# Banded tap matrices loaded from memory instead of built on GpSimd, and the modulation's dot products moved

## The chip, the cores and the metric

The kernel runs on one core of a Trainium2 chip. The metric is the device time of one execution in microseconds. Engines are named as in the profile: PE is TensorE (matmuls), PEld its weight load, DVE VectorE, ACT ScalarE, POOL GpSimd, SP SyncE, whose queue issues nearly all transfers from memory.

## The reference

Two layers over 512 latent tokens of 1024 features; each layer is a token mixer and a SwiGLU feed-forward block. The mixer of layer 0 is a gated linear attention that also reads 256 context tokens, the mixer of layer 1 a convolution module. Every sub-layer is normalised and modulated by vectors that come from the condition `c`.

```python
for i in range(2):
    mod_lat = silu(c) @ w_mod[i] + b_mod[i]          # 6 vectors of 1024
    sh1, sc1, gt1, sh2, sc2, gt2 = split(mod_lat, 6)
    h = modulate(rmsnorm(x, norm_mix_g[i]), sh1, sc1)
    y = gla(h, h_ctx) if i == 0 else conv_module(h)
    x = x + gt1 * y
    x = x + gt2 * swiglu(modulate(rmsnorm(x, norm_ffn_g[i]), sh2, sc2), w_in[i], w_out[i])
return rmsnorm(x, final_norm_g)

def conv_module(h):                                  # 31 taps, one filter per channel
    u = h @ w_pw1 + b_pw1
    u = u[:, :1024] * sigmoid(u[:, 1024:])
    u = depthwise_conv(u, w_dw) + b_dw
    return silu(layernorm(u)) @ w_pw2 + b_pw2
```

## The kernel before

Activations lie transposed: 8 tiles `x` of 128 features by 512 tokens. Every matrix product is done in three matmuls (`mm3`, L95 to L97): weights and activations are split into a rounded high part and the rest (`wh`, `wl`; for activations `hi`, `lo`), high times high, high times rest, rest times high. A weight chunk of 128x1024 comes by one transfer into a raw tile `wr` (three buffers), ACT casts it to `wh` (L110), DVE subtracts to get `wl` (L111); `wh` and `wl` have four buffers each. SP issues transfers in program order, and one that waits for its buffer holds back those behind it.

The order of stages is: start and attention (to about 320 us), its output projection, the feed-forward block of layer 0 (`ffn(0)`: 22 pairs of column blocks in `pairs`, then `out_proj`), the convolution module, and the feed-forward block of layer 1 (`ffn(1)`). `ffn(0)` is ordered by a scheduler, the convolution by lists written by hand (`mix`).

Between two stages stands a norm. When the tokens of one half (256) are complete, `rstd_y` sums squares on PE (L158), DVE turns the sums into reciprocal roots by eight tiny instructions on 128x2 elements (L164 and, in `newton`, L183 to L190), PE spreads them over partitions (`spread`, L170), and DVE with ACT makes the next stage's input: L197 (input times scale, the spread value read from PSUM), ACT L198, DVE L199 (which makes the low part from two tiles in SBUF). Then the other half follows. The last of `out_proj`'s eight column blocks is done in halves, so that the first half's norm can run beside the second half's matmuls.

The modulation vectors are dot products on DVE: `mod_jobs` is a generator whose every step multiplies one loaded 128x1024 tile `wm` of `w_mod` with `silu(c)` and accumulates into a column of `dots` (L229), then loads the next tile into the only `wm` buffer. After every eighth dot POOL adds the bias (L233). `step(n)` takes n steps; before, `ffn(0)` calls `step(3)` after each of 20 pairs, until none is left.

In the convolution, three of eight channel tiles (`PCH` = 4, 5, 6) are convolved on PE. For this each needs 36 banded 128x128 matrices of taps; four lie in one 128x512 tile, so there are 9 tiles a channel tile and 27 in all. Before, POOL builds them right after `ffn(0)` (L1128) by multiplying a mask of 32 diagonals (`m32`) with the taps (`wph`), one instruction for each tile:

```python
pool.tensor_tensor(tt.rearrange("p (a b) -> p a b", b=32), m32.unsqueeze(1).to_broadcast([P, 16, 32]),
                   w.unsqueeze(2).to_broadcast([P, 16, 32]), op=ALU.mult)
```

The tiles take buffers of kind `s`, of which `ffn(0)` has used all 36 until its `out_proj` has read them. PE reads the matrices in `pe_lane`, from about 820 us on.

Of the kernel before, what the change touches and what calls it, by code (L numbers as in the profile page):

```python
# [7 lines left out]
F32 = mybir.dt.float32  # L8
# [8 lines left out]
ALU = mybir.AluOpType  # L17

P = 128
D = 1024  # L20
KC = D // P
SEQ = 512
CTX = 256
HID = 2816
HC = HID // P
# [9 lines left out]
PCH = (4, 5, 6)  # L35
NF = 4
NSH = 9
# [18 lines left out]
def hybrid_kernel(ctx: ExitStack, tc: tile.TileContext, t: dict):  # L56
    nc = tc.nc
    act, dve, pool, pe, sp = nc.scalar, nc.vector, nc.gpsimd, nc.tensor, nc.sync

    cst = ctx.enter_context(tc.tile_pool(name="cst", bufs=1))  # L60
# [25 lines left out]
    def bt(tag, dt=F32):  # L86
        if tag in "cd":
            return wide(tag, dt)[:, 2:514]
        return big.tile([P, 512], dt, tag=tag, bufs=NBUF[tag], name=nm(tag))
# [127 lines left out]
    def mod_jobs():  # L217

        ij = [(0, j) for j in range(16, 48)] + [(1, j) for j in range(48)]

        def load(i, j):
            raw = wts.tile([P, 1024], F32, tag="wm", bufs=1, name=nm("wm"))
            sp.dma_start(raw, t["wmod"][i, j])
            return raw
        raw = load(*ij[0])
        yield
        for n, (i, j) in enumerate(ij):
            o = i * 48 + j
            dve.scalar_tensor_tensor(raw, raw, 1.0, sil, op0=ALU.mult, op1=ALU.mult, accum_out=dots[:, o:o + 1])  # L229
            if n + 1 < len(ij):  # L230
                raw = load(*ij[n + 1])
            if j % 8 == 7:
                pool.tensor_tensor(mod[i][:, j - 7:j + 1], dots[:, o - 7:o + 1],  # L233
                                   col(C_BMOD + o - 7, 8), op=ALU.add)
            yield

# [2 lines left out]
    def step(n):  # L239
        for _ in range(n):  # L240
            if next(jobs, 0) == 0:
                return
# [695 lines left out]
            if beside:  # L938
                beside(i)

    def ffn(i, h_, gt2, nx, after):
        sT = []

        def evac(j, po, c0, c1):
            n = c1 - c0
            if c0 == 0:
                tag = "s" if j < 18 else "c" if j < 20 else "d"
                sT.append((bt(tag, F32R), bt(tag, F32R)))
            hi, lo = sT[j]
            a = bt("t")  # L950
            act.activation(a[:, :n], po[0][:, :n], AF.Silu)
            dve.tensor_tensor(a[:, :n], a[:, :n], po[1][:, :n], op=ALU.mult)  # L952
            act.copy(hi[:, c0:c1], a[:, :n])  # L953
            dve.tensor_tensor(lo[:, c0:c1], a[:, :n], hi[:, c0:c1].bitcast(F32), op=ALU.subtract)

        pairs(f"wf{i}", HC, h_, evac, lambda i: step(3))
        r = resid(gt2)

        def ev2(m, p_, c0, c1):
            r(m, p_, c0, c1)  # L960
            nx.add(m, xs[m], c0, c1)

        out_proj(f"wo{i}", HC, sT, ev2, nx.tail, after)

# [14 lines left out]

    def after2(hf):  # L980
        if hf == 0:
            step(100)
            make_a(acol[:, 24:32], mod[1][:, 8:16], col(C_GMIX + 8, 8))
            make_a(acol[:, 32:40], mod[1][:, 32:40], col(C_GFFN + 8, 8))
        in2(hf)

    ffn(0, in1.h, mod[0][:, 40:48], n2, after2)


    HALF = WID // 2  # L990
# [128 lines left out]

    toep, ug, pe_ps, scr = {}, {}, {}, {}  # L1120

    def toeplitz(m, tag="s"):

        c = (m - PCH[0]) * 4 * NSH * NF
        for i in range(0, 4 * NSH, 4):
            tt = bt(tag)
            w = wph[:, c + i * NF:c + (i + 4) * NF]
            pool.tensor_tensor(tt.rearrange("p (a b) -> p a b", b=32), m32.unsqueeze(1).to_broadcast([P, 16, 32]),  # L1128
                               w.unsqueeze(2).to_broadcast([P, 16, 32]), op=ALU.mult)
            for j in range(4):  # L1130
                toep[m, (i + j) // NSH, (i + j) % NSH] = tt[:, j * P:(j + 1) * P]

# [184 lines left out]
    def bias2(k):  # L1317
        act.activation(xs[k], xs[k], AF.Identity, bias=gb2[:, k:k + 1])
# [32 lines left out]
            ev3(m, p_, *halves[hf])  # L1351

    ev3 = closing(mod[1][:, 16:24], n3)
    m32 = cst.tile([P, 32], F32, name="m32")
    sp.dma_start(m32, t["m32"])
    bph = cst.tile([P, 4 * len(PCH)], F32, name="bph")
    sp.dma_start(bph, t["bph"])
    wph = bt("g")
    sp.dma_start(wph[:, :len(PCH) * 4 * NSH * NF], t["wph"])
    for m in range(KC):  # L1360
        if m in PCH:
            toeplitz(m)
        else:
            cv_new(m)
    uw = {0: pair_load(0), 1: pair_load(1)}
    prod = wts.tile([P, 1024], F32, tag="wm", bufs=1, name=nm("wm"))
# [2 lines left out]
    with tc.manual_schedule(engines={E.Activation, E.DVE, E.Pool, E.PE}):  # L1369
        pool_lane = pool_order()  # L1370
        dve_start, dve_lane = dve_order()
        warm(AF.Sigmoid)
        po.update({(i, h): pair_mm(uw[i], *h) for h, i in ((h0, 0), (h0, 1), (h1, 0))})
        evc(0, po[0, h0], *h0)
        mix(dve_start[0],
            at=[(0.4, lambda: evc(1, po[1, h0], *h0)), (0.7, lambda: uw.update({2: pair_load(2)}))])
        evc(0, po[0, h1], *h1)
        po[1, h1] = pair_mm(uw[1], *h1)
        po[2] = pair_mm(uw[2], 0, SEQ)
        mix(take(pool_lane, 5), dve_start[1], at=[(0.7, lambda: evc(1, po[1, h1], *h1))])  # L1380
        for p in range(1, 7):
            def evac():
                if p > 1:
                    need(ORD[p])
                    po[ORD[p + 1]] = pair_mm(uw[p + 1], 0, SEQ, range(4))

            def second():
                if p > 1:
                    pair_mm(uw[p + 1], 0, SEQ, range(4, KC), po[ORD[p + 1]])

            def load():
                if p + 2 < KC:
                    uw[p + 2] = pair_load(ORD[p + 2])
            at = [(0.04, evac), (0.25, load), (0.5, second)]
            if p >= 3:
                at += [(0.6, lambda: bias2(2 * p - 6)), (0.8, lambda: bias2(2 * p - 5))]
            if p == 3:
                at += [(SH[0], shift_sums), (SH[1], shift_bc), (SH[2], shift_copy)]
            if p >= 5:
                at += [(0.3, lambda: to_groups(ORD[p]))]  # L1400
            mix(take(pool_lane, PN[p - 1]), take(dve_lane, DN[p - 1]), at=at)
        mix(pe_lane(4), take(pool_lane, PN[6]), take(dve_lane, DN[6]),
            at=[(N6, lambda: need(6)), (N6, lambda: to_groups(6)), (0.3, lambda: load2(0)), (0.7, lambda: load2(1))])
        pe_store(4)
        mix(pe_lane(5), take(pool_lane, PN[7]), take(dve_lane, DN[7]),
            at=[(0.3, lambda: load2(4, "s")), (0.9, lambda: pe_back(4, dve))])
        pe_store(5)
        warm(AF.Silu)
        mix(pe_lane(6), pool_lane, dve_lane, at=[(0.1, lambda: load2(2)), (0.2, lambda: load2(3))])
        cv_new(6)  # L1410
        pe_out(6, 0, act)
        pe_out(6, 1, act)
        pool.tensor_tensor(cv[6][0:64], cv[6][0:64], ncb[0:64], op=ALU.add)
        ln_open()
        pe_out(6, 2, dve)
        pe_out(6, 3, dve)
        pe_back(5, act)
        ks = (1, 0, 2, 3, 4, 7, 5, 6)
        for k in ks:
            run(ln_sums(k, 0, k == ks[-1]))  # L1420
        b = [f for k in ks for f in ln_sums(k, 1, k == ks[-1])]
        run(take(b, S1))
        ln_stat(0)
        ln_bc(0)
        run(take(b, S2))
        lane = ln_lane(0)
        run(take(lane, 5))

        def rest():
            run(b)  # L1430
            run(lane)
            ln_stat(1)
        first = pw2(range(4), 0, {1: rest, BC: lambda: ln_bc(1)})
        load2(5, "s")
        lane = ln_lane(1)
        run(take(lane, L1))
        pw2_out(first, 0)
        run(lane)
        pw2_out(pw2((4, 5), 0), 0)
        pw2_out(pw2(range(4), 1), 1)  # L1440
        load2(6)
        load2(7)
        pw2_out(pw2((4, 5), 1), 1)
# [16 lines left out]
            (sp, act)[k // 2 % 2].dma_start(t["out"][k:k + 2, :, c0:c1].rearrange("k p c -> p k c"),  # L1460
                                            y.rearrange("p (k c) -> p k c", k=2))

    ffn(1, in3.h, mod[1][:, 40:48], n4, final)

# [14 lines left out]
def phases(w):  # L1481

    import numpy as np
    pad = NF * MID + NF - 1 - WID // 2
    wp = np.pad(w, ((pad, pad), (0, 0)))
    r, d, f = np.ogrid[:NF, :NSH, :NF]
    a = wp[NF * d + r - f + NF - 1].reshape(NF, NSH, NF, KC, 4, 32)[:, :, :, list(PCH)]
    return np.ascontiguousarray(a.transpose(0, 5, 3, 4, 1, 2)).reshape(P, -1)


def layout(x, c, ctx, c_ctx, w_mod, b_mod, norm_mix_g, norm_ffn_g, gla_w_in, gla_wa_f, gla_ba_f,
# [4 lines left out]
    a = {}  # L1496
# [21 lines left out]
    tt = np.arange(512)  # L1518
    a["pmask"] = np.ascontiguousarray((np.arange(P)[:, None] > (tt % P)[None]).astype(f32))
    a["ident"] = np.eye(P, dtype=f32)  # L1520
    a["m32"] = np.ascontiguousarray(np.tile(np.eye(32, dtype=f32), (4, 1)))
    b = conv_b_dw[0].reshape(KC, 4, 32)[list(PCH)].reshape(-1, 32).T
    a["bph"] = np.ascontiguousarray(np.tile(b, (NF, 1)))
    a["wph"] = phases(conv_w_dw[0])
    a["wgo"] = _units(gla_w_out[0])
    a["wp1"] = _pairs(conv_w_pw1[0])
    a["wp2"] = _units(conv_w_pw2[0])
# [21 lines left out]
```

## Time and profile before

| | us |
|---|---|
| three runs: median (lowest, highest) | 1287.11 (1284.47, 1287.29) |
| the profiled execution, its own time | 1287.67 |
| its span from first to last instruction | 1285.7 |
| PE busy in it | 1234.1 |
| DVE busy | 734.7 |
| ACT busy | 475.8 |
| POOL busy | 226.9 |

The profiled execution's time is 1.97 us above its span and 0.56 us above the median of the runs. PE is busy nearly all the time, so a gain can come only from the places where it waits or where its clock is low; those are found by stretch, not by the sums over the whole.

### The profile page before, as it was taken

What the parts mean: (1) busy time and instruction counts of PE and PEld (TensorE: products, weight loads), DVE (VectorE), ACT (ScalarE), POOL (GpSimd) and SP (SyncE); (2) the same over time, 40 slices, a digit from 0 to 9 for tenths busy, and PEclk for the clock granted to TensorE, in tenths of its full rate; (3) what the DMA queues carried; (4) which work ended last, traced back from release to release, by engine and by line L of the source; (5) the groups of instructions that cost most, each with busy time, mean ns of one, the idle gap of its engine ahead of it and who ended that gap; (6) DMA issues with size and microseconds to landing.
All of it is one profiled execution on the core that took longest, in us unless ns stands there. A gap on an engine that the chain in (4) does not pass through costs nothing.

```text
span 1285.7 us, 17000 instructions
## 1 busy us (share of the span) xinstructions
PE 1234.1 (96%) x6692; PEld 1069.6 (83%) x6692; DVE 734.7 (57%) x1279; ACT 475.8 (37%) x748; POOL 226.9 (18%) x191
## 2 busy tenths in 40 slices
PE   8899899999899999999999699999999999999997
PEld 7678799898898888877888598889988888888886
DVE  2997976747775545545532889986733333332223
ACT  3245655443342222222222368855422222222220
POOL 0032211122200000000011859933000000000110
PEclk7999999999899999999999899999999999999999
DMA  7642542235456666556633123321143333333321
GB/s 277 223 132 74 164 147 83 83 99 149 141 167 196 193 186 196 194 166 205 195 112 101 50 66 95 117 85 65 55 128 99 97 95 95 93 95 100 93 72 66
DMA packets 54180, 162.34 MB, mean 126 GB/s; under 512 B 6226, under 2 KB 12242, under 8 KB 54100
## 3 DMA queue, kind: packets, MB, share of 16 engines
q1 hardware_dynamic: 52436, 159.16, 39.8%
q10 hardware_dynamic: 1664, 2.10, 0.5%
q8 instruction: 52, 0.85, 0.3%
q14 instruction: 28, 0.23, 0.1%
HBM read 157.83 MB, written 3.41 MB: 125 GB/s over the span
## 4 chain that ended last, share of the span: by engine, by line
PE 67%; DVE 16%; DMA 9%; issue 4%; ACT 3%; POOL 0%; DVEq 0%; ACTq 0%; POOLq 0%
PE pm L95 18%; PE pm L97 18%; PE pm L96 18%; DMA wm<-wmod 8%; DVE g L253 3%; DVE pa L1088 2%; DVE wl L111 2%; DVE wm L229 2%; PE pm L366 1%; PE pm L367 1%; PE pm L368 1%; ACT wh L110 1%; PE pa L620 1%; PE pm L527 1%; DVE pm L1088 1%
## 5 line engine op out<-in xcount | busy, mean ns | idle before, releaser
L97 PE MATMUL pm<-h,wl 128*128 128x512 f32 (+1 forms) x1008 | 373.3, 372 | 4.9 <-DVE wl L111 2.8
L96 PE MATMUL pm<-h,wh 128*128 128x512 f32 (+1 forms) x1008 | 372.1, 371 | 2.8 <-DVE h L199 2.8
L95 PE MATMUL pm<-h,wh 128*128 128x512 f32 (+1 forms) x1008 | 371.9, 372 | 0.2 <-ACT wh L110 0.2
L111 DVE TENSOR_TENSOR wl<-wr,wh 128x1024 fp32r<-128x1024 f32 (+1 forms) x176 | 224.6, 1280 | 256.9 <-ACT wh L110 255.0
L110 ACT CAST wh<-wr 128x1024 fp32r<-128x1024 f32 (+2 forms) x197 | 200.3, 1025 | 421.6 <-PE pm L96 398.8
L97 PEld LDWEIGHTS pm<-h,wl 128*128 128x128 f32 x1008 | 191.0, 190 | 39.2 <-DVE wl L111 4.4
L96 PEld LDWEIGHTS pm<-h,wh 128*128 128x128 f32 x1008 | 191.1, 190 | 35.2 <-DVE h L199 3.4
L95 PEld LDWEIGHTS pm<-h,wh 128*128 128x128 f32 x1008 | 190.1, 190 | 31.7 <-ACT wh L110 0.7
L95 PE MATMUL pm<-s,wh 128*128 128x512 f32 (+1 forms) x540 | 187.2, 347 | 1.1 <-ACT s L1271 1.1
L96 PE MATMUL pm<-s,wh 128*128 128x512 f32 (+1 forms) x540 | 186.8, 346 | 0.3 <-DVE s L278 0.2
L97 PE MATMUL pm<-s,wl 128*128 128x512 f32 (+1 forms) x540 | 186.0, 345 | 0.0
L229 DVE SCALAR_TENSOR_TENSOR wm<-wm,sil 128x1024 f32<-128x1024 f32 x80 | 102.0, 1275 | 129.1 <-DMA wm<-wmod 129.0
L885 POOL TENSOR_TENSOR g<-g,g 128x512 f32<-128x512 f32 (+1 forms) x31 | 39.8, 1283 | 488.4 <-ACT g L883 487.6
L96 PEld LDWEIGHTS pm<-s,wh 128*128 128x128 f32 x540 | 103.6, 192 | 13.1 <-DVE s L278 0.9
L95 PEld LDWEIGHTS pm<-s,wh 128*128 128x128 f32 x540 | 103.6, 192 | 13.2 <-ACT s L1271 1.3
L97 PEld LDWEIGHTS pm<-s,wl 128*128 128x128 f32 x540 | 103.6, 192 | 11.8
L111 POOL TENSOR_TENSOR wl<-wr,wh 128x1024 fp32r<-128x1024 f32 x21 | 53.1, 2541 | 198.7 <-ACT wh L110 198.7
L233 POOL TENSOR_TENSOR mod<-dots,cols 128x8 f32<-128x8 f32 x10 | 4.4, 443 | 277.6 <-DVE wm L229 277.6
L1088 DVE SCALAR_TENSOR_TENSOR pa<-s,cols,pa 128x503 f32<-128x503 f32 (+18 forms) x80 | 52.8, 701 | 0.6
L898 DVE SCALAR_TENSOR_TENSOR x<-pm,mod,x 128x256 f32<-128x256 f32 (+1 forms) x44 | 25.7, 601 | 47.5 <-PE pm L97 47.5
L953 ACT CAST s<-t 128x512 fp32r<-128x512 f32 (+1 forms) x40 | 23.1, 578 | 48.2 <-DVE t L952 48.2
L366 PE MATMUL pm<-wh,h 128*128 128x256 f32 x128 | 37.0, 289 | 0.0
(266 smaller groups left out, 1588.2 us busy)
## 6 DMA issues: line engine op xcount, KB each, us to landing
wr<-wf SPq DMA_DIRECT2D x88, 512.0 KB, 4.3
wm<-wmod SPq DMA_DIRECT2D x80, 512.0 KB, 3.7
wr<-wo SPq DMA_DIRECT2D x32, 512.0 KB, 3.7
wr<-wp SPq DMA_DIRECT2D x24, 512.0 KB, 3.9
s<-wmod SPq DMA_DIRECT2D x24, 256.0 KB, 5.5
wr<-wv SPq DMA_DIRECT2D x12, 512.0 KB, 4.1
wr<-wo SPq DMA_DIRECT2D x16, 384.0 KB, 3.3
wr<-wgo SPq DMA_DIRECT2D x8, 512.0 KB, 4.0
```

Of the source, the lines that this page charges most:

```text
L95: pe.matmul(out, wh, xh, start=start, stop=False)
L96: pe.matmul(out, wh, xl, start=False, stop=False)
L97: pe.matmul(out, wl, xh, start=False, stop=stop)
L110: act.copy(hi[:, :n], raw[:, :n])
L111: lo_eng.tensor_tensor(lo[:, :n], raw[:, :n], hi[:, :n].bitcast(F32), op=ALU.subtract)
L229: dve.scalar_tensor_tensor(raw, raw, 1.0, sil, op0=ALU.mult, op1=ALU.mult, accum_out=dots[:, o:o + 1])
L253: dve.scalar_tensor_tensor(junk, wt, 1.0, vec, op0=ALU.mult, op1=ALU.mult, accum_out=dsum[:, o:o + 1])
L366: pe.matmul(o, a, wh[:, w], start=k == 0, stop=False)
L885: pool.tensor_tensor(self.acc[:, c0:c1], self.acc[:, c0:c1], s[:, c0:c1], op=ALU.add)
L898: dve.scalar_tensor_tensor(xs[m][:, c0:c1], p_[:, :c1 - c0], gate[:, m:m + 1], xs[m][:, c0:c1], op0=ALU.mult, op1=ALU.add)
L953: act.copy(hi[:, c0:c1], a[:, :n])
L1088: dve.scalar_tensor_tensor(p_[:, lo:hi], u_sb[m][:, lo + s:hi + s], wcol(m, j), p_[:, lo:hi], op0=ALU.mult, op1=ALU.add)
```

## The change

Four things. (1) The 27 tiles of banded matrices are laid out in memory on the host (`banded`) and loaded by SP, 256 KB each, nine at a time after the pairs p = 1, 2 and 3 of the convolution; POOL's 27 multiplications, the mask and the compact taps go. (2) The modulation's bias is added by DVE and no longer by POOL. (3) `ffn(0)` calls `step(2)` after each pair and `step(1)` after each block of its `out_proj`, in place of `step(3)` and a final `step(100)`. (4) The last eight dot products, those of the second feed-forward's gate, are done in `ffn(1)`, one after each of eight pairs; their tiles come through the ring of three raw weight buffers `wr`.

```diff
         for n, (i, j) in enumerate(ij):
             o = i * 48 + j
+            if (i, j) >= (1, 40):
+                raw = load_raw(t["wmod"][i, j])
             dve.scalar_tensor_tensor(raw, raw, 1.0, sil, op0=ALU.mult, op1=ALU.mult, accum_out=dots[:, o:o + 1])
-            if n + 1 < len(ij):
+
+            if n + 1 < len(ij) and ij[n + 1] < (1, 40):
                 raw = load(*ij[n + 1])
             if j % 8 == 7:
-                pool.tensor_tensor(mod[i][:, j - 7:j + 1], dots[:, o - 7:o + 1],
+                dve.tensor_tensor(mod[i][:, j - 7:j + 1], dots[:, o - 7:o + 1],
                                    col(C_BMOD + o - 7, 8), op=ALU.add)
...
-        pairs(f"wf{i}", HC, h_, evac, lambda i: step(3))
+        pairs(f"wf{i}", HC, h_, evac, beside)
...
+            if beside2 and c0 == 0:
+                beside2()
...
-            step(100)
...
-    ffn(0, in1.h, mod[0][:, 40:48], n2, after2)
+    bph = cst.tile([P, 4 * len(PCH)], F32, name="bph")
+    sp.dma_start(bph, t["bph"])
+
+    ffn(0, in1.h, mod[0][:, 40:48], n2, after2, lambda i: step(2), lambda: step(1))
...
-    def toeplitz(m, tag="s"):
-
-        c = (m - PCH[0]) * 4 * NSH * NF
+    def toeplitz(m):
+
         for i in range(0, 4 * NSH, 4):
-            tt = bt(tag)
-            w = wph[:, c + i * NF:c + (i + 4) * NF]
-            pool.tensor_tensor(tt.rearrange("p (a b) -> p a b", b=32), m32.unsqueeze(1).to_broadcast([P, 16, 32]),
-                               w.unsqueeze(2).to_broadcast([P, 16, 32]), op=ALU.mult)
+            tt = bt("s")
+            sp.dma_start(tt, t["toep"][PCH.index(m), i // 4])
...
     for m in range(KC):
-        if m in PCH:
-            toeplitz(m)
-        else:
+        if m not in PCH:
             cv_new(m)
...
+            if p <= len(PCH):
+                at += [(0.35, lambda: toeplitz(PCH[p - 1]))]
...
-    ffn(1, in3.h, mod[1][:, 40:48], n4, final)
+    ffn(1, in3.h, mod[1][:, 40:48], n4, final, lambda i: step(1))
```

The order of PE's and ACT's instructions is the same in both kernels. That of three others moves.

POOL, from the end of `ffn(0)` to the first sum of the convolution, before (`g` are sums of squares, `s` the banded tiles, `m` the mask, `c` and `d` the convolution's outputs):

```order
L885 TENSOR_TENSOR g_5131<-g_5131,g_5575 128x512
L885 TENSOR_TENSOR g_5131<-g_5131,g_5664 128x512
L1128 TENSOR_TENSOR s_5968<-m_5950,g_5954 128x512
...
L1128 TENSOR_TENSOR s_5986<-m_5950,g_5954 128x512
L1052 COPY c_5956<-ones 128x2
```

and now:

```order
L888 TENSOR_TENSOR g_5085<-g_5085,g_5544 128x512
L888 TENSOR_TENSOR g_5085<-g_5085,g_5636 128x512
L1060 COPY c_5927<-ones 128x2
L1061 COPY c_5927<-ones 128x2
L1060 COPY c_5930<-ones 128x2
```

All 27 multiplications are gone from between the last sum of squares and the first addition of the convolution.

SP, in the convolution, before: only the weights `wp` of the first pointwise product, two chunks for each pair.

```order
L101 DMA wr_6369<-wp 128x1024
L101 DMA wr_6435<-wp 128x1024
L101 DMA wr_6441<-wp 128x1024
L101 DMA wr_6528<-wp 128x1024
L101 DMA wr_6534<-wp 128x1024
```

Now (the first and last of each group of nine):

```order
L101 DMA wr_6286<-wp 128x1024
L101 DMA wr_6370<-wp 128x1024
L1134 DMA s_6295<-toep 128x512
...
L1134 DMA s_6311<-toep 128x512
L101 DMA wr_6376<-wp 128x1024
L101 DMA wr_6481<-wp 128x1024
L1134 DMA s_6386<-toep 128x512
...
L1134 DMA s_6402<-toep 128x512
L101 DMA wr_6487<-wp 128x1024
```

The first group stands between the two chunks of pair 4, the second between those of pair 5, and the third behind the second chunk of pair 5, ahead of pair 6.

DVE, near the end of `ffn(0)`'s pairs, before (L111 a weight's low part, L229 a dot product, L952 and L954 the evacuation of a pair):

```order
L954 TENSOR_TENSOR s_4730<-t_4731,s_4729 128x512
L111 TENSOR_TENSOR wl_4833<-wr_4830,wh_4832 128x1024
L229 SCALAR_TENSOR_TENSOR wm_4580,dots<-wm_4580,sil 128x1024
L111 TENSOR_TENSOR wl_4905<-wr_4902,wh_4904 128x1024
L229 SCALAR_TENSOR_TENSOR wm_4584,dots<-wm_4584,sil 128x1024
L952 TENSOR_TENSOR t_4810<-t_4810,pm_4759 128x512
L111 TENSOR_TENSOR wl_4911<-wr_4908,wh_4910 128x1024
```

and now:

```order
L957 TENSOR_TENSOR s_4685<-t_4686,s_4684 128x512
L231 SCALAR_TENSOR_TENSOR wm_4918,dots<-wm_4918,sil 128x1024
L231 SCALAR_TENSOR_TENSOR wm_4921,dots<-wm_4921,sil 128x1024
L111 TENSOR_TENSOR wl_4851<-wr_4848,wh_4850 128x1024
L955 TENSOR_TENSOR t_4762<-t_4762,pm_4711 128x512
L111 TENSOR_TENSOR wl_4857<-wr_4854,wh_4856 128x1024
```

The two dots of a pair now stand together, behind the evacuation, and none is left between the two low parts of one pair. Until `out_proj`'s first block is added to `x` there are 48 dots of this generator in `ffn(0)` now, and 51 before.

## Rows read from the trace of the kernel before

**Rows 1.** The page: busy time by engine, and POOL's busy tenths in 40 slices.

```profile
PE 1234.1 (96%) x6692; PEld 1069.6 (83%) x6692; DVE 734.7 (57%) x1279; ACT 475.8 (37%) x748; POOL 226.9 (18%) x191
...
POOL 0032211122200000000011859933000000000110
```

**Rows 2.** The page: the chain of work that ended last, by line.

```profile
PE pm L95 18%; PE pm L97 18%; PE pm L96 18%; DMA wm<-wmod 8%; DVE g L253 3%; DVE pa L1088 2%; DVE wl L111 2%; DVE wm L229 2%; PE pm L366 1%; PE pm L367 1%; PE pm L368 1%; ACT wh L110 1%; PE pa L620 1%; PE pm L527 1%; DVE pm L1088 1%
```

**Rows 3.** PE's waits, 690 to 760 us: total, times, longest.

```profile
PE pa L170 <- DVE sm L190: 9.2, 2, 5.1
PE pm L96 <- DVE h L199: 2.8, 3, 2.3
```

**Rows 4.** Windows: length; busy (instructions) of PE, PEld, DVE, ACT, POOL; granted clock; DMA.

```profile
708.00:710.00 2.00, 0.15 (x2) 0.00 (x0) 1.93 (x3) 0.00 (x0) 2.00 (x3) 1.00 0.00 0
...
734.00:736.00 2.00, 0.00 (x0) 0.00 (x0) 1.93 (x3) 0.00 (x0) 2.00 (x3) 0.50 0.00 0
...
738.00:740.00 2.00, 2.00 (x11) 2.00 (x11) 2.00 (x4) 1.15 (x3) 2.00 (x3) 0.50 0.03 8
...
742.00:744.00 2.00, 2.00 (x19) 2.00 (x18) 2.00 (x7) 1.31 (x3) 0.00 (x0) 1.00 0.00 0
```

**Rows 5.** Timeline of DVE, 690 to 765 us: start, length.

```profile
706.54 0.16 DVE L164 TENSOR_SCALAR sm<-pa 128x2 f32<-128x2 f32 x1 [1.43 <-PE pa L158]
...
712.25 0.97 DVE L190 SCALAR_TENSOR_TENSOR sm<-sm,sm 128x2 f32<-128x2 f32 x1
714.54 1.26 DVE L197 SCALAR_TENSOR_TENSOR t<-x,acol,pa 128x256 f32<-128x256 f32 x3 [1.31 <-PE pa L170]
...
728.81 1.26 DVE L199 SCALAR_TENSOR_TENSOR h<-t,mod,h 128x256 fp32r<-128x256 f32 x1
...
735.05 0.97 DVE L190 SCALAR_TENSOR_TENSOR sm<-sm,sm 128x2 f32<-128x2 f32 x1
737.33 1.27 DVE L197 SCALAR_TENSOR_TENSOR t<-x,acol,pa 128x256 f32<-128x256 f32 x3 [1.31 <-PE pa L170]
```

**Rows 6.** Timeline of POOL, the same stretch.

```profile
705.13 10.08 POOL L1128 TENSOR_TENSOR s<-m,g 128x512 f32<-128x512 f32 x10 [5.15 <-PE pm L96]
...
724.31 17.08 POOL L1128 TENSOR_TENSOR s<-m,g 128x512 f32<-128x512 f32 x15
```

**Rows 7.** Timeline of DVE at the norm ahead of `ffn(1)`.

```profile
903.67 0.16 DVE L164 TENSOR_SCALAR sm<-pa 128x2 f32<-128x2 f32 x1 [1.72 <-PE pa L158]
...
905.05 0.16 DVE L190 SCALAR_TENSOR_TENSOR sm<-sm,sm 128x2 f32<-128x2 f32 x1
906.02 1.27 DVE L197 SCALAR_TENSOR_TENSOR t<-x,acol,pa 128x256 f32<-128x256 f32 x3 [0.80 <-PE pa L170]
...
919.80 1.26 DVE L197 SCALAR_TENSOR_TENSOR t<-x,acol,pa 128x256 f32<-128x256 f32 x3 [2.50 <-PE pa L170]
```

**Rows 8.** PE's waits, 460 to 700 us.

```profile
PE pm L97 <- DVE wl L111: 2.8, 2, 2.0
```

**Rows 9.** Timeline of DVE in the pairs of `ffn(0)`.

```profile
554.90 1.23 DVE L229 SCALAR_TENSOR_TENSOR wm<-wm,sil 128x1024 f32<-128x1024 f32 x1 [2.01 <-DMA wm<-wmod]
...
556.66 1.22 DVE L111 TENSOR_TENSOR wl<-wr,wh 128x1024 fp32r<-128x1024 f32 x1
```

**Rows 10.** Windows at the start, in the convolution and in `ffn(1)`: the last number is GB/s.

```profile
0.00:20.00 20.00, 16.40 (x66) 12.17 (x67) 3.31 (x11) 9.16 (x16) 2.57 (x9) 0.84 0.89 319
...
820.00:840.00 20.00, 20.00 (x168) 19.53 (x167) 19.96 (x27) 14.70 (x25) 19.84 (x17) 1.00 0.44 123
...
980.00:1000.00 20.00, 20.00 (x90) 16.57 (x89) 5.45 (x7) 4.73 (x7) 0.00 (x0) 1.00 0.34 105
```

**Rows 11.** The page's DMA issues, SP's timeline and ACT's: one chunk of pair 4.

```profile
wr<-wp SPq DMA_DIRECT2D x24, 512.0 KB, 3.9
...
762.65 0.33 SPq L101 DMA_DIRECT2D wr<-wp  x1
...
771.43 2.00 ACT L110 CAST wh<-wr 128x1024 fp32r<-128x1024 f32 x2
```

More of the change, by code (lines that the diff above doesn't have):

```diff
@@ L939, in pairs, with ffn @@
                 beside(i)
-    def ffn(i, h_, gt2, nx, after):
+    def ffn(i, h_, gt2, nx, after, beside, beside2=None):
         sT = []
@@ L1353, in hybrid_kernel @@
     ev3 = closing(mod[1][:, 16:24], n3)
[L1354 to L1359, printed above, removed]
     for m in range(KC):
-        if m in PCH:
-            toeplitz(m)
-        else:
+        if m not in PCH:
             cv_new(m)
@@ L1488, in phases, with banded @@
     return np.ascontiguousarray(a.transpose(0, 5, 3, 4, 1, 2)).reshape(P, -1)
+def banded(w):
+    import numpy as np
+    ph = phases(w).reshape(P, len(PCH), NSH, 4 * NF)
+    a = np.zeros((len(PCH), NSH, P, 4 * NF, 32), np.float32)
+    for p in range(P):
+        a[:, :, p, :, p % 32] = ph[p]
+    return a.reshape(len(PCH), NSH, P, SEQ)
 def layout(x, c, ctx, c_ctx, w_mod, b_mod, norm_mix_g, norm_ffn_g, gla_w_in, gla_wa_f, gla_ba_f,
@@ L1520, in layout @@
     a["ident"] = np.eye(P, dtype=f32)
-    a["m32"] = np.ascontiguousarray(np.tile(np.eye(32, dtype=f32), (4, 1)))
     b = conv_b_dw[0].reshape(KC, 4, 32)[list(PCH)].reshape(-1, 32).T
     a["bph"] = np.ascontiguousarray(np.tile(b, (NF, 1)))
-    a["wph"] = phases(conv_w_dw[0])
+    a["toep"] = banded(conv_w_dw[0])
     a["wgo"] = _units(gla_w_out[0])
```

## The prediction

> **What bounds the kernel now.** I read the busy times first: PE is busy 1234.1 of 1285.7 us [rows 1], so the whole is PE's, and only places where PE stands still or runs slowly can give anything back. The chain of work that ended last names, behind PE's own lines, the loads of modulation tiles with 8% [rows 2]: somewhere a dot product's transfer was the last to end. Then the windows. PE is full through the convolution and `ffn(1)` [rows 10]; it has holes at the start, at the norms between stages, and two small ones late in `ffn(0)`. The deepest is the passage from `ffn(0)` to the convolution, 708 to 741 us, and it is where the change takes POOL's 27 multiplications away.
>
> In that passage PE waits 9.2 us in two pieces for L190, the last instruction of the reciprocal root, and 2.8 us for L199 [rows 3]. With PE idle the granted clock falls: it is at 0.50, the 1.2 GHz level, in 734 to 736 and still in 738 to 740, where PE is fully busy but gets through 11 matmuls in 2 us against 19 at the 2.4 GHz level in 742 to 744 [rows 4]. The reason that L190 is late stands in the timeline of DVE: the root takes from 706.54 to 713.22, and each tiny instruction of it 0.97 us [rows 5]. POOL's multiplications run just then, ten in 10.08 us and fifteen in 17.08 us, so 1.0 and 1.1 us each [rows 6]: DVE gets one instruction through for each of POOL's. At the norm ahead of `ffn(1)`, where POOL is idle, the same eight instructions take 903.67 to 905.21, 1.54 us, and 0.16 each [rows 7]. L199 is stretched as well: one alone takes 1.26 us at 728.81 [rows 5], where three together take about as long elsewhere.
>
> The Trainium skill, page "SBUF — State Buffer", section "Who interferes with whom", says that a VectorE instruction with two inputs in SBUF and a GpSimd instruction that reads SBUF use one port, and that whoever comes second stands until the first is done. The row agrees as to which instructions suffer (the root and L199 have two SBUF inputs); the sum below uses only the durations.
>
> **First term: the passage.** The 27 multiplications are removed from POOL, nothing takes their place there before the first addition of the convolution, and PE's order is unchanged. So I replay the passage with the unstretched durations. First root: L164 at 706.54 as before, done at 706.54 + 1.54 = 708.08, where it was 713.22: 5.14 us. PE had just run dry then (0.15 us busy in 708 to 710 [rows 4]), so its spread follows without a hole. The first L197 comes 906.02 − 903.67 = 2.35 us behind L164, at 708.9 instead of 714.54.
>
> From there to the first L197 of the second half lie eight L197, eight L199, three weight subtractions, one addition to `x` and the second root. Before it took 737.33 − 714.54 = 22.8 us [rows 5]. I have two estimates of the unstretched length. The same passage ahead of `ffn(1)` took 919.80 − 906.02 = 13.8 us [rows 7]. Summing instructions (an L197 or L199 is 1.26 / 3 = 0.42 us, 17 of such size 7.1; the subtractions 3.5 at 1.2 [rows 9]; the small ones 1.5) and adding about 2.3 us of waits for PE's sums, ACT and the spread gives 14.4. I take 14.3, so the second half starts at 723.2, not 737.33: 14.1 us. Behind it, the half clock goes: some 4 us of matmuls ran at 11 for 19, which is 4 × (1 − 11/19) = 1.7 us; I take 1.5, because a short hole stays. First term: 15.6 us. Bounds: if PE never idled again, its 9.2 + 2.8 = 12.0 us of waits and about 5 us at half clock (three pieces like the one costed) come back, 17. If only the two roots shorten and the rest finds other waits, 5.1 + 4.8 = 9.9.
>
> Is the gain kept? PE is full, and at the full clock, from 742 to beyond 840 [rows 4, 10], so what follows shifts with PE. DVE and POOL are nearly full as well (19.96 and 19.84 of 20 us in 820 to 840 [rows 10]), but their lists begin on PE's results and begin earlier by as much; neither gets more work there.
>
> **Second term: the dots in `ffn(0)`.** Late in its pairs PE waits 2.8 us, twice, for a weight's low part [rows 8]. At the first, DVE stood 2.01 us for a tile of `w_mod`, did that dot from 554.90, and only then the subtraction that PE wanted, at 556.66 [rows 9]. The new order has no dot between the two subtractions of a pair. Moved ahead of that dot, the low part is ready by about 553, some 2 us before PE asks. The new DVE order still has two dots a pair, each behind its own load, so `step(2)` itself relieves little; what helps is where they stand, and 48 instead of 51 in the stretch. I take 2.8 us, bounds 0 and 2.8.
>
> **What costs nothing, and its cover.** The bias on DVE: ten instructions on 128x8, priced by the root's 0.16 us each [rows 7], 1.6 us in all over 600 us in which DVE has slack. The eight late dots in `ffn(1)`: DVE is busy 5.45 of 20 us there and DMA runs at 105 GB/s [rows 10]; a pair is 48 matmuls, 20 × 48 / 90 = 10.7 us, and needs of DVE two subtractions (2.4), an evacuation (about 1.4), the dot (1.23) and the wait for a 512 KB transfer, 3.9 [rows 11]: 8.9 us. In this ring the transfer of a dot is issued only when a slot is given back, so DVE does stand for it, with the next subtractions queued behind; but those are wanted a whole pair later. If the cover were gone, eight pairs could each lose up to their excess over 10.7 us; at a landing of 6 us that is 8 × 0.3, 2.4 us.
>
> The 27 loads: nine are 2.36 MB. At the 319 GB/s of the start, which has transfers of the same 256 KB, a group takes 7.4 us; at the 123 GB/s that the convolution moved, 19 [rows 10]. Behind the first group waits the second chunk of pair 4. Before, it was issued at 762.65, about 9.7 us after the first; it landed 3.9 us later and was cast second in a piece from 771.43 to 773.43, so at about 772.4 [rows 11]: 5.8 us to spare. A group may thus last 9.7 + 5.8 = 15.5 us before it costs anything. I take the upper rate, since 123 was what was asked for and not a limit, and so zero.
>
> On the same point the Trainium skill, page "SBUF — State Buffer", section "Summary: rules for kernel authors", asks for one transfer and not several, and "DMA: Bandwidth & Descriptors" gives a transfer about 2.0 us of fixed cost. Were the 27 to run one after another, that would add an estimated 54 us of queue time and hold the weights back; no row here shows loads of this queue in such a file.
>
> **Sum.** 15.6 + 2.8 = 18.4 us off the profiled execution: 1287.67 − 18.4 = 1269.3. That execution was 0.56 above the median of the runs, so I say 1269.0.
>
> **Rivals.** (a) New waits in the passage: ACT's casts or the sums on PE set the pace once DVE is free, and only the two roots come back: 1287.1 − 9.9 = 1277. For it: DVE waits for ACT and PE inside this passage. Against: the one ahead of `ffn(1)` did it in 13.8 us.
> (b) The bands hold back the weights, which ends slower: above 15.5 us a group each of three groups delays PE. At 100 GB/s a group lasts 23.6 us, 3 × 8.1 = 24 us, 1269 + 24 = 1293. Decided at 2.36 MB / 15.5 us = 152 GB/s. Against: 319 at the start.
> (c) POOL is not what stretches DVE, and the change doesn't do what it says: the second term alone, 1284.3. Against: the 0.16 and 0.97 us of the same instruction.
> (d) The late dots stall `ffn(1)`: 2 to 6 us, 1271 to 1275.
>
> **How the numbers follow.** The forecast (1265.5 to 1273) 0.68; (a) 0.15; (d) 0.05; (c) 0.05; (b) 0.03; better than 1265.5, 0.04. The range runs from the upper bound of the first term with all of the second (1287.1 − 17 − 2.8 = 1267.3, less a measurement's scatter) to (a): 1265.5 to 1277.5. About 0.3%, 3.9 us, is what a measurement of this kernel can tell. Case (c) is 0.2% and counts mostly as no change; so faster 0.92, same 0.05, slower 0.03.
>
> **What the profile would show.** Right: L183 to L190 at 0.16 us at every norm; the second half's first L197 about 14 us behind the first; the clock at 1.00 through the passage; no PE wait for L111 in `ffn(0)`; PE as full as before from there to the end. Wrong: PE waiting for L111 or ACT's cast in the convolution while the bands land, or in the first eight pairs of `ffn(1)`.

## The result, and the profile after

| | before | after |
|---|---|---|
| median of the runs beside each other, us | 1287.2 | 1265.66 (1263.12 to 1270.32) |
| the profiled execution, its own time | 1287.67 | 1270.32 |
| its span | 1285.7 | 1268.5 |

The changed kernel is faster: the ratio of the runs' times is 0.9842, 95% interval 0.9807 to 0.9876, so 16 to 25 us. The same kernel again (a1) gave 0.9841 (0.9806 to 0.9875, median 1266.49). The page after, busy times, POOL's slices and the chain of work that ended last:

```profile
PE 1231.4 (97%) x6692; PEld 1068.6 (84%) x6692; DVE 721.6 (57%) x1289; ACT 476.1 (38%) x748; POOL 192.5 (15%) x154
...
POOL 0033211112300000000011169913000000000110
...
PE pm L95 22%; PE pm L96 22%; PE pm L97 22%; DVE g L256 3%; DVE pa L1096 2%; DVE wl L111 2%; PE pm L370 1%; PE pm L369 1%; PE pm L371 1%; DMA wm<-wmod 1%; ACT wh L110 1%; PE pa L623 1%; PE pm L530 1%; DVE pm L1096 1%; DVE t L276 1%
```

PE's sum is nearly what it was [rows 1]: nearly all the time came out of its pauses, not its work. The loads of modulation tiles, 8% of the chain before [rows 2], are 1% of it; 8% of the span would be 103 us, so a share of this chain is not what its removal gives back.

The passage from `ffn(0)` to the convolution in the timeline of DVE (start, length), which answers to [rows 5]; the first row is from the attention and is taken up at e9:

```profile
246.35 2.20 DVE L190 SCALAR_TENSOR_TENSOR sm<-sm,sm 128x4 f32<-128x4 f32 x1
...
705.94 0.16 DVE L164 TENSOR_SCALAR sm<-pa 128x2 f32<-128x2 f32 x1 [1.43 <-PE pa L158]
...
707.32 0.16 DVE L190 SCALAR_TENSOR_TENSOR sm<-sm,sm 128x2 f32<-128x2 f32 x1
708.28 1.27 DVE L197 SCALAR_TENSOR_TENSOR t<-x,acol,pa 128x256 f32<-128x256 f32 x3 [0.81 <-PE pa L170]
...
718.21 0.16 DVE L183 TENSOR_SCALAR sm<-sm 128x2 int32<-128x2 int32 x1
...
721.75 1.26 DVE L197 SCALAR_TENSOR_TENSOR t<-x,acol,pa 128x256 f32<-128x256 f32 x3 [0.81 <-PE pa L170]
```

The first L197 comes 2.34 us behind L164, and the second half's first L197 13.47 us behind that one. PE's waits in 690 to 760 us, and windows that answer to [rows 4], with one from the attention (taken up further below), one from `ffn(0)` and one where bands load:

```profile
PE pm L96 <- DVE h L199: 0.4, 1, 0.4
```

```profile
160.00:164.00 4.00, 4.00 (x23) 4.00 (x23) 2.73 (x9) 2.95 (x8) 0.00 (x0) 0.57 0.58 216
...
708.00:710.00 2.00, 2.00 (x20) 2.00 (x19) 1.72 (x4) 1.55 (x3) 0.00 (x0) 1.00 0.04 8
734.00:736.00 2.00, 2.00 (x19) 2.00 (x18) 2.00 (x3) 0.79 (x2) 0.00 (x0) 1.00 0.19 37
...
460.00:700.00 240.00, 240.00 (x1074) 198.98 (x1073) 109.76 (x143) 64.33 (x80) 10.01 (x6) 1.00 0.49 157
740.00:760.00 20.00, 20.00 (x90) 16.56 (x89) 17.71 (x21) 14.95 (x22) 18.90 (x15) 1.00 0.92 322
```

In the passage PE now waits 0.4 us in all for DVE and the granted clock stays at 1.00 (the 2.4 GHz level), and behind it 322 GB/s of bands and weights pass beside a full PE. Where the time went, from the starts of L164 at the norms in DVE's timeline (the length of a stage is the difference of two of them):

| stage | before | after | difference |
|---|---|---|---|
| start and attention, to the norm ahead of `ffn(0)` | 337.37 | 340.80 | +3.4 |
| `ffn(0)`, to the norm behind it | 369.17 | 365.14 | −4.0 |
| passage and convolution, to the norm ahead of `ffn(1)` | 197.13 | 180.65 | −16.5 |
| `ffn(1)`, to the last norm | 363.84 | 363.85 | 0.0 |

The first row was in nobody's sum; it is taken up below.

### The profile page after: what moved, and what is told of

It is laid out like the page before. It is cut to its first block, busy times and chain, and to the rows that moved or that the text cites. A ratio compares the mean times of both kernels' runs of the same rounds, so it can differ in the third digit from the quotient of the medians.

```text
span 1268.5 us, 17022 instructions
## 1 busy us (share of the span) xinstructions
PE 1231.4 (97%) x6692; PEld 1068.6 (84%) x6692; DVE 721.6 (57%) x1289; ACT 476.1 (38%) x748; POOL 192.5 (15%) x154
## 4 chain that ended last, share of the span: by engine, by line
PE 77%; DVE 14%; issue 4%; ACT 3%; DMA 1%; POOL 1%; DVEq 0%; ACTq 0%; POOLq 0%
PE pm L95 22%; PE pm L96 22%; PE pm L97 22%; DVE g L256 3%; DVE pa L1096 2%; DVE wl L111 2%; PE pm L370 1%; PE pm L369 1%; PE pm L371 1%; DMA wm<-wmod 1%; ACT wh L110 1%; PE pa L623 1%; PE pm L530 1%; DVE pm L1096 1%; DVE t L276 1%
## 5 line engine op out<-in xcount | busy, mean ns | idle before, releaser
L111 DVE TENSOR_TENSOR wl<-wr,wh 128x1024 fp32r<-128x1024 f32 (+1 forms) x176 | 221.1, 1260 | 244.7 <-ACT wh L110 242.8
L231 DVE SCALAR_TENSOR_TENSOR wm<-wm,sil 128x1024 f32<-128x1024 f32 x72 | 93.9, 1304 | 108.4 <-DMA wm<-wmod 108.2
L111 POOL TENSOR_TENSOR wl<-wr,wh 128x1024 fp32r<-128x1024 f32 x21 | 52.6, 2517 | 215.4 <-ACT wh L110 200.6
L369 PE MATMUL pm<-wh,h 128*128 128x256 f32 x128 | 37.0, 289 | 0.0
L371 PE MATMUL pm<-wl,h 128*128 128x256 f32 x128 | 36.2, 283 | 0.0
L370 PE MATMUL pm<-wh,h 128*128 128x256 f32 x128 | 36.2, 283 | 0.0
```

Source lines behind the costliest of these rows:

```text
L111: lo_eng.tensor_tensor(lo[:, :n], raw[:, :n], hi[:, :n].bitcast(F32), op=ALU.subtract)
L369: pe.matmul(o, a, wh[:, w], start=k == 0, stop=False)
L370: pe.matmul(o, b, wh[:, w], start=False, stop=False)
L371: pe.matmul(o, a, wl[:, w], start=False, stop=k == KC - 1)
```

## The experiments

Times are medians beside runs of the kernel before on the same chip (1284.5 to 1286.5 there); ratios are those of all the runs. Stage lengths are from each run's own trace, read as in the table.

**e1: bands loaded, nothing else.** The kernel before, with part 1 of the change alone.

```diff
-            pool.tensor_tensor(tt..., m32..., w..., op=ALU.mult)
+            sp.dma_start(tt, t["toep"][PCH.index(m), i // 4])
```

> The kernel before with part 1 alone: bands loaded, none built. My theory (the multiplications on POOL stretch the two roots and what follows them, and the idle PE then loses its clock): the roots at 0.16 us an instruction, the second half's first L197 13 to 14 us behind the first, and 15 to 17 us off, about 1271. The two stalls of PE for a low part late in ffn(0), 2.8 us in all, stay. Rival (c), POOL does not stretch DVE: about 1287, unchanged. Rival (b), the bands hold back the weights: above 1287, with PE waiting for L111 or a cast in the convolution.

Measured: 1267.88, ratio 0.9847 (0.982 to 0.9875). The passage is that of the changed kernel (180.66 us, roots at 0.16). But the stalls in `ffn(0)` did not stay: that stage took 365.32 us, with the order of before on every engine there. The window:

```profile
460.00:700.00 240.00, 240.00 (x1081) 199.24 (x1080) 115.29 (x152) 62.51 (x77) 11.61 (x11) 1.00 0.54 173
```

240.00 of 240 us. So the 2.8 us of [rows 8] are not in every execution.

**e2: everything but the bands.** The changed kernel with POOL's multiplications, mask and taps restored.

> The changed kernel with the bands built by POOL again, so parts 2 to 4 alone (bias on DVE, dots spread, eight of them late). My theory: ffn(0) without its stalls for low parts, 3 to 4 us off, about 1283.5; roots at 0.97 us an instruction and the passage as long as before. If the dots' places were worth nothing: 1287. If the late dots cost time in ffn(1): above 1287 or a stage ffn(1) longer than 363.8 us.

Measured: 1282.15, ratio 0.9971 (0.995 to 0.9993). Roots at 0.97 us, passage 197.8 us; `ffn(0)` 365.30, `ffn(1)` 363.8. Parts 2 to 4 together are worth 1 to 6 us, the bands the rest.

**e4: multiplications that nobody reads.** The changed kernel, and the 27 multiplications in their old place, into tiles without a reader.

```diff
+            for i in range(0, 4 * NSH, 4):
+                tt = bt("s")
+                w = wph[:, c + i * NF:c + (i + 4) * NF]
+                pool.tensor_tensor(tt..., m32..., w..., op=ALU.mult)
```

> The changed kernel with the 27 multiplications back on POOL in their old place, into tiles that nobody reads; the loaded bands are used. My theory: nothing waits for the multiplications, they only disturb DVE: the roots go back to about 1 us an instruction, the granted clock falls again in the passage, and most of the 16 us is lost, 1279 to 1283. Rival: the gain came from PE or the convolution no longer waiting for the built bands, or for their buffers, and the multiplications in themselves harm nothing: stays at 1266.

Measured: 1281.86, ratio 0.9972 (0.9951 to 0.9993): 16 us lost. PE's waits in 690 to 760 us:

```profile
PE pa L170 <- DVE sm L190: 9.8, 2, 5.1
PE pm L96 <- DVE h L199: 2.8, 3, 2.3
```

These are the two waits of [rows 3]. The bands are loaded here, so nothing waited for the built ones; POOL's work beside DVE is enough. Rival (c) falls. The multiplications of e4 still take 27 tiles of kind `s`, so this run alone doesn't separate their work from their hold on buffers; e10 does, whose memsets take the same tiles and cost nothing.

**e5: POOL only writes.** As e4, with two memsets for each multiplication: nearly as much time on POOL (0.5 us each against 1.0 to 1.1), and nothing read.

```diff
+                tt = bt("s")
+                pool.memset(tt, 0.0)
+                pool.memset(tt, 0.0)
```

> The changed kernel with 54 memsets on POOL in the old place (two for each of 27 tiles that nobody reads), which write as many bytes or more but read none. If POOL harms DVE by reading the memory from which DVE's two inputs come: roots at 0.16 us, passage as without them, about 1266. If any work of POOL does it: roots near 1 us and 1279 to 1283 as with the multiplications, as far as the memsets last as long. Between the two, a slower root by a part tells of a port shared by writes.

Measured: 1283.26, ratio 0.9972 (0.9949 to 0.9994), as slow as e4, but neither theory had the reason. DVE's timeline and POOL's, from the two roots:

```profile
705.77 0.32 DVE L183 TENSOR_SCALAR sm<-sm 128x2 int32<-128x2 int32 x1
...
717.99 13.68 DVE L183 TENSOR_SCALAR sm<-sm 128x2 int32<-128x2 int32 x1
718.05 13.61 DVE L111 TENSOR_TENSOR wl<-wr,wh 128x1024 fp32r<-128x1024 f32 x1
719.19 12.48 DVE L199 SCALAR_TENSOR_TENSOR h<-t,mod,h 128x256 fp32r<-128x256 f32 x1
...
732.68 0.16 DVE L190 SCALAR_TENSOR_TENSOR sm<-sm,sm 128x2 f32<-128x2 f32 x1
```

```profile
705.07 0.99 POOL L1364 MEMSET s<- 128x512 f32 x2
706.01 1.01 POOL L1363 MEMSET s<- 128x512 f32 x2
...
718.03 0.99 POOL L1363 MEMSET s<- 128x512 f32 x2
...
731.59 0.19 POOL L1060 COPY d<-ones 128x2 f32<-128x2 f32 x1
```

The first half ran almost as if POOL were idle, though the memsets ran beside it: L183 took 0.32 us and the rest of its root 0.16 each, as L190 of the second root does at 732.68. But in the second root L183, the root's only instruction whose one input is a tile in SBUF (L164 reads PSUM), did not end until the memsets paused at 731.6; L111 and L199 behind it end at the same moment, and PE waited 12.4 us for that L199.

**e10: the same, L183 with two inputs.** L183 takes its constant from a tile instead of an immediate.

```diff
-        dve.tensor_scalar(y.bitcast(I32), v.bitcast(I32), scalar1=-0.5, scalar2=MAGIC, ...)
+        dve.scalar_tensor_tensor(y.bitcast(I32), v.bitcast(I32), -0.5, mag[:, :nblk], ...)
```

> The kernel with the 54 memsets, but L183, the first instruction of the root, takes its constant from a tile, so that it too has two inputs in memory and is a SCALAR_TENSOR_TENSOR like those behind it. In the memset kernel every instruction with two inputs ran undisturbed beside the memsets, and L183, with one input, stood 13.68 us. Theory A (a writing POOL harms no two-input instruction, and the one-input form of L183 was what could not get past the memsets): no instruction of the second root is stretched, no wait of 12 us for L199, and about 1266. Theory B (L183 was caught by chance, or whatever instruction stands there is caught by the memsets that follow one another without a gap): 1280 to 1284 again, with 12 us or so of wait in the passage.

Measured: 1264.85, ratio 0.9835 (0.9796 to 0.9873). The 54 memsets cost nothing. DVE's timeline (L185 is L183 here, L191 is L190) and POOL's beside it:

```profile
710.84 0.15 DVE L185 SCALAR_TENSOR_TENSOR sm<-sm,mag 128x2 int32<-128x2 int32 x1
710.91 1.22 DVE L111 TENSOR_TENSOR wl<-wr,wh 128x1024 fp32r<-128x1024 f32 x1
...
713.41 0.16 DVE L191 SCALAR_TENSOR_TENSOR sm<-sm,sm 128x2 f32<-128x2 f32 x1
```

```profile
710.99 0.99 POOL L1364 MEMSET s<- 128x512 f32 x2
...
712.87 0.99 POOL L1364 MEMSET s<- 128x512 f32 x2
```

Theory A holds. L111, which ended together with L183 in e5, takes its usual 1.22 us here, so it was L183 that stood. With e4, the pair says that POOL's multiplications stretch DVE's two-input instructions and POOL's memsets do not. That it is the reading which makes the difference is the nearest explanation and not shown alone: a memset is also another instruction, half as long. The Trainium skill, "SBUF — State Buffer", section "Who interferes with whom", says just that (a VectorE instruction with two inputs in SBUF contends with a GpSimd instruction that reads SBUF, not with one that only writes), and there too that `tensor_scalar` can enter a mode that takes the shared pair of ports, and can then contend, when its operands meet certain conditions. This pair of runs agrees as to which instructions suffer (0.16 us for the two-input ones beside the memsets, 13.68 us for L183); which mode L183 ran in, no run shows.

**e3 and b1: the order of before in `ffn(0)` again.** e3 is the kernel before with part 2 alone; b1 is the kernel before once more.

```diff
-                pool.tensor_tensor(mod[i][:, j - 7:j + 1], ...
+                dve.tensor_tensor(mod[i][:, j - 7:j + 1], ...
```

> The kernel before with part 2 alone: the modulation's bias added by DVE. My theory: no difference, 1287 (within 1 us either way), the roots still at 0.97 us. It is also a second look at the dots of before in ffn(0): the kernel with the loaded bands alone had the same order on DVE there and no stall for a low part, so the 2.8 us may have been one execution's late transfer. Theory of the prediction: the stalls at 550 to 600 us are there again, stage ffn(0) 369 us. Rival: they are chance, and the stage takes 365.3 us as in that kernel. Rival: POOL's ten additions held up DVE, and 3 to 4 us are gained.

> The kernel before once more, for a further look at ffn(0). If the stalls for a weight's low part come with the three dots a pair, PE waits there again, for 1 to 3 us, and the stage takes 367 to 369 us; the two other looks at this order had 1.6 and none. Passage 197 us and the roots at 0.97 us, as before.

Measured: e3 1287.97, ratio 1.0018 (0.9998 to 1.0037), so the bias is worth nothing. PE's waits in 345 to 700 us, of e3 and then of b1 (which took 1290.39 in its one run):

```profile
PE pm L97 <- DVE wl L111: 1.6, 2, 1.4
```

```profile
PE pm L97 <- DVE wl L111: 1.8, 2, 1.2
```

With [rows 8] and e1, three dots a pair stalled PE for 2.8, 1.6, 1.8 and 0 us, and the stage took 369.2, 367.6, 367.8 and 365.3; in the ten profiles with two dots a pair it took 364.9 to 365.3, without such a wait. Both pictures were half right: the order makes the stall possible, and the execution decides whether it comes.

**e8: the late dots back.** The last eight dots at the end of `ffn(0)`.

```diff
-            if (i, j) >= (1, 40):
-                raw = load_raw(t["wmod"][i, j])
...
+            step(100)
```

> The changed kernel with the last eight dots done at the end of ffn(0) again and not in ffn(1). My theory: they cost nothing in ffn(1), which keeps its 363.85 us, and little at the end of ffn(0): 1266, or up to 3 us more if they hold up the last halves there. Rival (d): ffn(1) gets 2 to 6 us shorter, 1261 to 1264.

Measured: 1269.93, ratio 0.9869 (0.9842 to 0.9896); `ffn(0)` 365.29, the passage and convolution 180.60, `ffn(1)` 363.84, all as with the late dots. Neither place costs anything that the traces show; the intervals of the ratios overlap, so the medians' difference may be scatter. Rival (d) falls.

**e6 and e7: bands loaded twice and three times.** Each group of nine is followed by one or two repetitions of its loads, into the same tiles. The longer groups also change SP's order at one place: in both traces one weight chunk stands between the first and the second group and two between the second and the third, where the changed kernel has two and one.

```diff
+        for r in range(1):        # e7: range(2)
+            for i, tt in enumerate(tts):
+                sp.dma_start(tt, t["toep"][PCH.index(m), i])
```

> The changed kernel with every band tile loaded twice, so 18 loads of 256 KB in each group. My theory: a group takes about 14.7 us at the 322 GB/s of the nine-load groups, just below the 15.5 us of cover, and the time stays at 1266 (to 1268). Rival (b), a queue that cannot carry them: every group delays PE, at 123 GB/s by 38 - 15.5 = 23 us each, 1335.

> The changed kernel with every band tile loaded three times, 27 loads in each group. My theory: a group takes about 22 us and has 15.5 us of cover, so PE waits 6.5 us at each of three groups for the low part of the second weight chunk: 1266 + 20 = 1286, a little less if the slack carries over. Rival: the cover is larger than I worked out, and the time stays at 1266.

Measured: e6 1268.44 (0.9868, 0.9838 to 0.9897), e7 1287.98 (1.0013, 0.9996 to 1.0031). The stage from the norm behind `ffn(0)` to that ahead of `ffn(1)` took 185.6 and 202.3 us against 180.65: 5.0 and 21.7 lost. In e7, ACT's casts wait for the chunks behind the groups, and PE runs dry:

```profile
757.97 1.04 ACT L110 CAST wh<-wr 128x1024 fp32r<-128x1024 f32 x1 [6.37 <-DMA wr<-wp]
777.52 1.04 ACT L110 CAST wh<-wr 128x1024 fp32r<-128x1024 f32 x1 [11.34 <-DMA wr<-wp]
...
798.39 1.04 ACT L110 CAST wh<-wr 128x1024 fp32r<-128x1024 f32 x1 [11.32 <-DMA wr<-wp]
```

```profile
760.00:780.00 20.00, 11.03 (x51) 8.89 (x51) 8.19 (x13) 7.60 (x12) 8.71 (x8) 0.88 1.05 389
```

So the mechanism of rival (b) exists, and its threshold lies between this load and twice it. In e6 the cast behind the first group waits 0.19 us for its chunk, those behind the second and the third 3.22 and 5.05 us:

```profile
748.04 1.06 ACT L110 CAST wh<-wr 128x1024 fp32r<-128x1024 f32 x1 [0.19 <-DMA wr<-wp]
...
762.05 1.05 ACT L110 CAST wh<-wr 128x1024 fp32r<-128x1024 f32 x1 [3.22 <-DMA wr<-wp]
...
776.66 1.05 ACT L110 CAST wh<-wr 128x1024 fp32r<-128x1024 f32 x1 [5.05 <-DMA wr<-wp]
```

The first group of 18 loads was thus covered and the next two were not: 15.5 us was read off the first, and behind it PE's demand goes on at one pair in about 10.7 us. Besides, the moved chunk adds to what waits behind the second group; how the loss divides between the two was not tried.

**e9 and a1: the same contention elsewhere.** Eight of the attention's weight subtractions go from POOL to DVE; a1 is the changed kernel again, beside it.

```diff
-            got.append(load_w(a, 1024, (pool, dve)[n]))
+            got.append(load_w(a, 1024, (pool if len(ld) <= 13 else dve, dve)[n]))
```

> The changed kernel with the last eight of the attention's 21 weight subtractions that POOL does (2.4 us each, from about 215 us on) done by DVE (1.2 us each). My theory: POOL's subtraction no longer stretches L190 at 246 us (2.20 us against 0.16), PE's waits for L190 there (2.5 us) and for POOL's low parts (1.9 us) go, and the eight subtractions lie in DVE's slack: 3 to 4 us off, 1262. Rival: DVE's list is what PE waits for in that stage, and each subtraction ahead of an L472 or L434 delays PE by up to 1.2 us: unchanged or up to 5 us slower.

> The changed kernel once more, for the scatter of its first stages and as the measure of the kernel beside it. From the runs so far 1266; the stage from the norm ahead of ffn(0) to the one behind it 365.1 to 365.3 us, the passage to the norm ahead of ffn(1) 180.7 us, and the start and attention anywhere between 331 and 341 us. If the low clock at 160 to 164 us belongs to the change, it is there again; if it is chance, it need not be.

Measured: e9 1262.21, ratio 0.981 (0.9777 to 0.9844); a1 1266.49, 0.9841 (0.9806 to 0.9875). The intervals overlap, so what e9 gains has to be read from the traces. In the changed kernel POOL's subtraction at 246 us met the root's L190, which took 2.20 us at 246.35 (shown with the profile after). POOL's timeline there, and DVE's in e9:

```profile
246.19 2.34 POOL L111 TENSOR_TENSOR wl<-wr,wh 128x1024 fp32r<-128x1024 f32 x1 [2.82 <-ACT wh L110]
```

```profile
239.01 0.16 DVE L190 SCALAR_TENSOR_TENSOR sm<-sm,sm 128x4 f32<-128x4 f32 x1
```

e9 reaches this place 7 us earlier than a1, so its window is moved by as much. e4, which has POOL's subtractions, reaches it nearly as early as e9 (its L190 takes 2.20 us at 239.53). The windows of a1, e4 and e9 in this order:

```profile
240.00:260.00 20.00, 17.49 (x86) 14.98 (x85) 15.87 (x27) 10.60 (x17) 6.04 (x3) 0.91 0.34 106
```

```profile
233.00:253.00 20.00, 17.48 (x99) 15.15 (x98) 15.87 (x27) 10.60 (x17) 5.70 (x3) 1.00 0.33 106
```

```profile
233.00:253.00 20.00, 20.00 (x120) 17.78 (x119) 16.77 (x32) 11.46 (x20) 0.00 (x0) 1.00 0.38 115
```

PE's wait of 2.5 us for L190 is gone in e9. The lower clock of a1 does not come from that wait alone, since e4 has the wait and 1.00. The 2.0 us for POOL's low parts stayed, against my expectation: none of PE's waits after 200 us in a1 is for them. e9 has the lowest median measured here, 4.3 us below a1; 2.5 us of that are shown. Its profile's start and attention, 329.9 us, is 10 us shorter than a1's but only 1.6 us shorter than e4's, and most of the 10 us belongs to the scatter of that stage (below).

## Why the prediction was right, and where it was off

**The first term** was right in cause and nearly in size. Its replay of the root gave 2.35 us from L164 to the first L197 (measured 2.34); the stretch to the second half was put at 14.3 us and took 13.47. The two give 5.7 + 9.3 = 15.0 us, where 5.6 + 8.5 = 14.1 were forecast; the stage as a whole gave 16.5, which leaves 1.5 for the clock, as priced. Against the four other profiles with POOL's multiplications (197.8 to 198.8 us in b1, e2, e3 and e4) the gain is 17 to 18 us, so 16.5 is at the low end. The 14.3 was too long because it favoured a sum of instructions with 2.3 us of waits over the row of the undisturbed passage, 13.8 [rows 7], which was the better guide. e4 and e10 show the cause: POOL's multiplications put back alone bring the loss, memsets in their place do not. The clock's part was right: no window of the passage falls below 1.00 after.

Three readings were loose. "Each tiny instruction of it 0.97 us" holds for six of the eight, and not all of the root has two inputs in SBUF. Three more rows of the trace before, all beside POOL's multiplications:

```profile
706.74 0.47 DVE L183 TENSOR_SCALAR sm<-sm 128x2 int32<-128x2 int32 x1
...
725.57 0.47 DVE L197 SCALAR_TENSOR_TENSOR t<-x,acol,pa 128x256 f32<-128x256 f32 x1
...
726.75 1.01 DVE L183 TENSOR_SCALAR sm<-sm 128x2 int32<-128x2 int32 x1
```

L183 has one SBUF input and was stretched all the same (0.17 and 0.16 us after), which e5 and e10 come back to. L164 (0.16 us) reads PSUM and L197 takes one input from SBUF and one from PSUM; neither was stretched. And "DVE gets one instruction through for each of POOL's" describes the rows but is no rule for POOL at work: e10 has two memsets for each multiplication, and DVE is not held up.

**The second term**, 2.8 us, was a stall that comes and goes. In four profiles of the old order the stage was longer than with the new one by 3.9, 2.3, 2.5 and 0 us (against 365.3), on average about 2. The term's size stands, its step did not say that one execution is one draw. (Moved ahead of the dot, the low part would have been ready at about 554.0 by the rows, not 553: the evacuation ahead of it ends at 552.9. The 2 us before PE asks are right.) The stage also gave more than PE's visible waits, 4.0 for 2.8; why is not shown.

**The zeros** held. Bias: e3, no gain. Late dots: e8 and the stage's 363.85 us. The 27 loads: 322 GB/s where the upper rate had been taken; but the cover of 15.5 us was read off the first group and used for all three, and e6, where 0 to 2 us were expected, lost 5.0.

**The sum**: 18.4 forecast; 16.5 + 4.0 = 20.5 by stages, 17.35 by the two profiled executions, and about 20 by the ratio. So the sum was some 2 us too small, the median of 1265.66 us is 3.3 below the forecast 1269.0 and only 0.16 above the lower end of the range, and a1's 1266.49 is 1.0 above it. That the profiled execution, 1270.32, came within about 1 us of its forecast 1269.3 is luck: between 20.5 and 17.35 lies, but for 0.3 us, the +3.4 of the table's first row, a stage in which the change moves only a few bias additions. Start and attention took 333.1 us in e6, 340.0 in a1 and 340.80 in the changed kernel's first profile, with the same instructions in the same order up to there; 331.6 in e4 and 333.3 in e10, which differ there by one small load and by L183 with its constant; and 337.37 and 339.34 in the two profiles of before. Part of the difference arises at the very start, while the first tiles are loaded: the first weight subtraction on DVE begins 3.1 us later in the changed kernel's first profile than in e6 (in this order):

```profile
26.92 1.09 DVE L111 TENSOR_TENSOR wl<-wr,wh 128x896 fp32r<-128x896 f32 x1
```

```profile
23.79 1.09 DVE L111 TENSOR_TENSOR wl<-wr,wh 128x896 fp32r<-128x896 f32 x1
```

Another part goes with low clock in short stretches. In the window 160 to 164 us the changed kernel has 0.57 (above), and b1, the kernel before:

```profile
160.00:164.00 4.00, 4.00 (x23) 4.00 (x23) 2.73 (x9) 3.00 (x9) 0.00 (x0) 0.59 0.64 201
```

The kernel before has it in this profile and not in its first (1.00); the changed kernel has it in both of its profiles, and e6 and e10, with its order up to there but for e10's L183, do not. So it isn't the change that brings it; what decides stays open.

## What to carry to other kernels

Where an engine's tiny instructions take about as long as another engine's large ones, and a fraction of that elsewhere in the same trace, the two engines probably share something: price the passage by replaying it with the undisturbed durations, and give PE's clock back as a term of its own. Look for the same pair of operations in other stages; here one line found it again in the attention (e9). Compare kernels stage by stage, take a second profile of a stall of one or two microseconds before giving it to an edit, and compare windows that hold the same work and not the same time.

## What the runs showed of the hardware

L183, a DVE instruction with one input in SBUF, stood 13.68 us behind a row of POOL memsets of about 0.5 us each, which followed one another without a gap: it was not let in between two of them. The root of the first half in the same run got past the same memsets in 0.32 us (both rows stand at e5). The second L183 had right behind it on DVE a two-input L111 that could start without its result, and the first had only the rest of its root, which could not; whether that matters was not tried. The memsets left the two-input instructions at 0.15 and 0.16 us (e10), and yet they are no safe neighbour for this one-input one; of other one-input instructions these runs don't speak.
